# Two activations in one moving operand, and hidden tiles at a new place: the up and down projections of an MLP in a two-layer trunk on one core

## The chip, the core and the metric

The kernel runs on one core of one Trainium2 chip. Its engines are TensorE (matmuls and the loads of their stationary operand, PE and PEld in the profile), VectorE (DVE), ScalarE (ACT), GpSimd (POOL) and SyncE (SP, which issues most DMAs). The metric is the time of one execution on the device in microseconds (us).

## The reference

Two decoder layers over 256 tokens of width 2048, all in float32. Layer 0 mixes with a state-space block and an SSD block, layer 1 with RWKV-7 and RG-LRU; each layer then has an MLP and a gated embedding. What matters here, with the rest left out:

```python
def squared_relu_mlp(h, w1, w2):            # w1: 2048 x 8192, w2: 8192 x 2048
    return jnp.square(jax.nn.relu(h @ w1)) @ w2
...
    for i in range(2):
        hn = rmsnorm(h, norm_mix[i])
        ...
        h = h + mix
        h = h + squared_relu_mlp(rmsnorm(h, norm_ffn[i]), mlp_w1[i], mlp_w2[i])
        gate = jax.nn.sigmoid(rmsnorm(h, norm_pl[i]) @ pl_gate[i])
        h = h + gate * (p[i] @ pl_proj[i])
    return rmsnorm(h, norm_final)
```

## The kernel before

Every matmul of the large products takes its operands in a rounded float32 format (`FR`). To keep float32 accuracy each operand is split into a high part, the rounded value, and a low part, the rest; a product is then three matmuls, high by high, high by low and low by high, added in PSUM. The split is `split`: a copy on ScalarE (line 172) makes the high part, a subtraction on VectorE (line 153) the low one.

Weights stream from HBM in tiles of 512 KB, 128 partitions by 1024 values: `wload` issues the DMA on SP's queue into one of three `raw` buffers, `wtile_` splits it into `wh` and `wl`, which have three buffers each in layer 0 (`wp0`) and six in layer 1 from the last output projection on (`wp3`). They are given a high priority when the order of ScalarE's and VectorE's instructions is fixed at build time; each engine then works through its own list in that order.

Two helpers hold most of the matmuls. In `gemm_ws` (lines 344 to 362) the weights are stationary, 128x128 at a time, and the activations move, 256 tokens: the result has features on partitions. The MLP's up projection uses it, 512 columns of W1 per call, in two PSUM banks of the tag `acc` (six banks in the MLP). In `gemm_as` (lines 322 to 342) an activation tile of 128x128 is stationary and 512 weight columns move: the result has tokens on partitions. The MLP's down projection (`project`), the projection of the per-layer input (operand `px`) and the embed gate use it.

`prep` (from line 364) transposes the residual on TensorE (line 370) and splits it into the tiles that the matmuls read (`t` in the profile, from the pool `s4`). `mlp` (from line 455) runs over eight pieces c of 1024 hidden features: `up(c)` calls `gemm_ws` twice, and after each call ScalarE takes relu and square, and the result is split into the tiles `hid`; then the piece before is projected down with `project(prev, ...)`, four chunks of 512 output columns, each added to the residual on VectorE. In c = 0, where there is nothing to project yet, `between()` prepares `px` after the two calls.

Pools lie in SBUF one behind the other, in the order in which they are opened. In the MLP of layer 0 the weights' pool `wp0` comes first, then `h0` (four 4 KB tiles of the residual, 288 and 96 bytes), `pl0` (two `pt` tiles of 1 KB and two `px` tiles of 2 KB) and `mlp0`, which begins with the small tile `r2`, followed by the `hid` tiles of 4 KB. In layer 1 `pl1` follows `wp3` directly, and then `mlp1`. The pools `s4` and the weights' are a multiple of 512 bytes apart.

Of the kernel before, what the change touches and what calls it, by code (L numbers as in the profile page):

```python
# [11 lines left out]
F32 = mybir.dt.float32  # L12
FR = mybir.dt.float32r
I32 = mybir.dt.int32
AF = mybir.ActivationFunctionType
OP = mybir.AluOpType
# [3 lines left out]
D = 2048  # L20
T = 256
FF = 8192
# [49 lines left out]
class K:  # L72
# [249 lines left out]
    def gemm_as(self, xs, W, r0, c0, nn=512, shared=False):  # L322

        nk = len(xs)
        if shared:
            q = self.acc([128, 2, nn])
            ps = [q[:, 0], q[:, 1]]
        else:
            ps = [self.acc([128, nn]) for _ in range(2)]
        step = 2 * 512 // nn  # L330
        f = dict(skip_group_check=True)
        for kb in range(0, nk, step):
            wh, wl = self.wtile(W, r0[kb] if isinstance(r0, list) else r0 + kb, step, c0, nn)
            for kk in range(step):
                k = kb + kk
                h, l = xs[k]
                for t in range(2):
                    s = slice(128 * t, 128 * t + 128)
                    self.nc.tensor.matmul(ps[t], h[:, s], wh[:, kk], start=k == 0 and not (shared and t), stop=False, **f)  # L339
                    self.nc.tensor.matmul(ps[t], h[:, s], wl[:, kk], start=False, stop=False, **f)  # L340
                    self.nc.tensor.matmul(ps[t], l[:, s], wh[:, kk], start=False, stop=k == nk - 1, **f)  # L341
        return ps

    def gemm_ws(self, xs, W, c0, ms):
        nk = len(xs)
        nn = sum(ms)
        step = 4 if nn <= 256 else 2
        ps = [self.acc([128, 2, T]) for _ in range((len(ms) + 1) // 2)]
        for kb in range(0, nk, step):
            wh, wl = self.wtile(W, kb, step, c0, nn)  # L350
            for kk in range(step):
                k = kb + kk
                h, l = xs[k]
                o = 0
                for m, mw in enumerate(ms):
                    out = ps[m // 2][:mw, m % 2, :]
                    f = dict(skip_group_check=True)
                    self.nc.tensor.matmul(out, wh[:, kk, o:o + mw], h, start=k == 0 and m % 2 == 0, stop=False, **f)  # L358
                    self.nc.tensor.matmul(out, wh[:, kk, o:o + mw], l, start=False, stop=False, **f)  # L359
                    self.nc.tensor.matmul(out, wl[:, kk, o:o + mw], h, start=False, stop=k == nk - 1, **f)  # L360
                    o += mw
        return ps

    def prep(self, src, g, j0, nj, alloc=None):

        hb, lb = ((alloc or self.t4)([128, nj, T], FR) for _ in range(2))
        for i in range(nj):
            q = self.pq([128, T])
            for t in range(2):
                self.nc.tensor.transpose(q[:, 128 * t:128 * t + 128], src(t, j0 + i), self.ident)  # L370
            if g is None:
                self.split(hb[:, i], lb[:, i], q)
            else:
                s = g(j0 + i)
                self.pa = self.act(hb[:, i], q, AF.Copy, scale=s)
                self.pv = self.stt(lb[:, i], q, s, hb[:, i].bitcast(F32), OP.mult, OP.subtract)
                self.pas.append((self.pa, self.pv))
        return [(hb[:, i], lb[:, i]) for i in range(nj)]

    def norm_prep(self, gname):  # L380

# [64 lines left out]

        self.project([x for y, _ in ys for x in self.split_y(y)], W, [r + i for _, r in ys for i in range(4)], **k)

    def project(self, xs, W, r0, scale=None, nn=512):
        for c0 in range(0, D, nn):  # L450
            ps = self.gemm_as(xs, W, r0, c0, nn, nn < 512)
            for t in range(2):
                self.add_h(t, c0, ps[t], None if scale is None else scale[:, t:t + 1], nn)


    def mlp(self, i, w1, w2, between):

        xs, rstd = self.norm_prep(f"gf{i}")

        def up(c):  # L460
            hs = []
            for nb in range(2):
                ps = self.gemm_ws(xs, w1, c * 1024 + nb * 512, [128] * 4)
                hh, hl = (self.l("hid", 8, [128, 4, T], FR) for _ in range(2))
                for a in range(2):
                    r = self.l("relu", 4, [128, 2, T])
                    self.act(r, ps[a], AF.Relu)
                    self.act(r, r, AF.Square)
                    self.split(hh[:, 2 * a:2 * a + 2], hl[:, 2 * a:2 * a + 2], r)
                hs += [(hh[:, j], hl[:, j]) for j in range(4)]  # L470
            return hs

        prev = None
        with self.scope(f"mlp{i}") as self.lp:
            r2 = self.l("r2", 1, [128, 2])
            self.tt(r2, rstd, rstd, OP.mult)
            for c in range(FF // 1024 + 1):
                cur = up(c) if c < FF // 1024 else None
                if c == 0:
                    between()  # L480
                if prev is not None:
                    self.project(prev, w2, 8 * (c - 1), r2)
                prev = cur

    def embed_prep(self, i, p, pool):
# [7 lines left out]
    def embed(self, i, px, W, Wg, out=None):  # L493
        with self.scope(f"embed{i}") as self.lp:
            es = []
            for nb in range(4):
                pp = self.gemm_as(px, W, 0, 512 * nb)
                for t in range(2):
                    e = self.l("pl", 8, [128, 512])
                    self.act(e, pp[t], AF.Copy)  # L500
                    es.append(e)
            xs, rstd = self.norm_prep(f"gp{i}")

            def gate(t, c0, nn, ps):
                with (self.tc.high_priority(100000) if c0 >= 1536 else ExitStack()):
                    g = self.t2([128, 512], name="gate")[:, :nn]
                    self.act(g, ps, AF.Sigmoid, scale=rstd[:, t:t + 1])
                    e = es[2 * (c0 // 512) + t][:, c0 % 512:c0 % 512 + nn]
                    self.tt(g, g, e, OP.mult)
                    self.add_h(t, c0, g, nn=nn)  # L510
                    if out is not None:
                        self.final_part(t, c0, nn)

            for c0, nn in GB[:len(GB) - (out is not None)]:
                ps = self.gemm_as(xs, Wg, 0, c0, nn)
                for t in range(2):
                    gate(t, c0, nn, ps[t])
            if out is not None:

                c0, nn = GB[-1]  # L520
                ws = [self.wtile(Wg, kb, 1024 // nn, c0, nn) for kb in range(0, 16, 1024 // nn)]
                for t in range(2):
                    ps = self.acc([128, nn])
                    for k in range(16):
                        h, l = (x[:, 128 * t:128 * t + 128] for x in xs[k])
                        wh, wl = (w[:, k % (1024 // nn)] for w in ws[k // (1024 // nn)])
                        self.nc.tensor.matmul(ps, h, wh, start=k == 0, stop=False)
                        self.nc.tensor.matmul(ps, h, wl, start=False, stop=False)
                        self.nc.tensor.matmul(ps, l, wh, start=False, stop=k == 15)
                    gate(t, c0, nn, ps)  # L530
                    self.final(t, out)
# [287 lines left out]
    def ssd_dt(self, xs, rstd, raw):  # L819
        nc = self.nc  # L820
        hl = self.wp.tile([128, 16, 48], FR, name="wh", tag="wh")
        self.split(hl[:, :, 0:24], hl[:, :, 24:48], raw)
        q = self.pm([48, T])
        for k in range(16):
            h, l = xs[k]
            f = dict(skip_group_check=True)
            nc.tensor.matmul(q, hl[:, k], h, start=k == 0, stop=False, **f)
            nc.tensor.matmul(q[0:24], hl[:, k, 0:24], l, start=False, stop=k == 15, **f)
        d = self.t4([48, T], name="d")
        self.act(d, q, AF.Copy)  # L830
        pd = self.pm([128, 2, 24])
        for t in range(2):
            nc.tensor.matmul(pd[:, t], d[:, 128 * t:128 * t + 128], self.sel.bitcast(F32), start=True, stop=True)
        n = 48
        x = self.c([128, 48], pool=self.lp)
        for t in range(2):
            self.stt(x[:, 24 * t:24 * t + 24], pd[:, t], rstd[:, t:t + 1], self.hp[:, 0], OP.mult, OP.add)
        return x
# [665 lines left out]
```

## Time and profile before

| | |
|---|---|
| time of three runs, us | 2599.24, 2602.3, 2596.33 (median 2599.24) |
| profiled execution, its own time, us | 2599.46 |
| span of its instructions, us | 2597.7 |
| mean granted TensorE clock | 0.992 |
| instructions | 41093 |

The profile records one execution. The span is the time from the first to the last instruction. An engine's busy time counts its records without overlap; matmul records overlap, and their ends are modelled, so the pace of a run of matmuls is the difference of two start times divided by the number of steps between. L358 to L360 are the three matmuls of `gemm_ws`, L339 to L341 those of `gemm_as`. In the records `acc<-t,wh` names the output and the inputs by tile.

### The profile page before, as it was taken

To read this page: it belongs to the slowest core of one execution; us is meant where nothing else is said; L and a number is where in the kernel's file an instruction comes from. 1 tells how busy PE (TensorE), PEld (TensorE's weight loads), DVE (VectorE), ACT (ScalarE), POOL (GpSimd) and SP (SyncE) were. 2 spreads that over 40 slices of the span, in tenths; PEclk is the share of its full clock that TensorE was granted. 3 is DMA by queue.
4 is the path that set the end of the run, shared out by engine and by line. 5 is a ranking of instruction groups with operands and counts; after the bars stand their busy time and mean duration, and the time that the engine had idled before them with its cause. 6 is when DMAs were issued, how large, how long until landed. Compare 5 with 4: busy or idle time off the path is not lost. (4 is left out here: it accounts for less than half of the span.)

```text
span 2597.7 us, 41093 instructions
## 1 busy us (share of the span) xinstructions
PE 2538.0 (98%) x16352; PEld 2284.7 (88%) x16352; DVE 1630.8 (63%) x2557; ACT 1301.1 (50%) x1885; POOL 119.6 (5%) x255
## 2 busy tenths in 40 slices
PE   7989999999999999999999999999999999999998
PEld 6878878988988998878899998889898899889787
DVE  7999866455455445566566789775555545554565
ACT  5454745444444444455455667555444444444464
POOL 4200010000000000000100010100000000000000
PEclk9999999999999999999999999999999999999999
DMA  6545345665666566556556525366656656666654
GB/s 199 157 126 157 119 140 166 182 187 187 184 184 187 184 187 186 186 178 203 160 149 174 150 73 157 98 195 195 187 179 186 191 185 185 187 186 180 190 180 139
DMA packets 262593, 443.27 MB, mean 171 GB/s; under 512 B 16768, under 2 KB 81408, under 8 KB 262400
## 3 DMA queue, kind: packets, MB, share of 16 engines
q1 hardware_dynamic: 256560, 431.25, 54.6%
q0 software_dynamic: 5696, 9.18, 1.3%
q8 instruction: 128, 2.10, 0.3%
q14 instruction: 65, 0.53, 0.1%
q10 hardware_dynamic: 144, 0.21, 0.0%
HBM read 435.34 MB, written 5.24 MB: 170 GB/s over the span
## 5 line engine op out<-in xcount | busy, mean ns | idle before, releaser
L153 DVE TENSOR_TENSOR wl<-raw,wh 128x1024 fp32r<-128x1024 f32 x810 | 990.6, 1224 | 803.1 <-ACT wh L172 802.5
L172 ACT ACTIVATE wh<-raw 128x1024 fp32r<-128x1024 f32 x811 | 856.6, 1057 | 1063.1 <-PE acc L341 522.0
L360 PE MATMUL acc<-t,wl 128*128 128x256 f32 x3136 | 895.4, 286 | 9.2 <-DVE wl L153 9.0
L358 PE MATMUL acc<-t,wh 128*128 128x256 f32 x3136 | 895.8, 286 | 1.5 <-ACT t L172 1.1
L359 PE MATMUL acc<-t,wh 128*128 128x256 f32 x3136 | 895.7, 286 | 0.0
L360 PEld LDWEIGHTS acc<-t,wl 128*128 128x128 f32 x3136 | 603.8, 193 | 12.8 <-DVE wl L153 11.2
L358 PEld LDWEIGHTS acc<-t,wh 128*128 128x128 f32 x3136 | 603.8, 193 | 4.3 <-ACT t L172 1.3
L359 PEld LDWEIGHTS acc<-t,wh 128*128 128x128 f32 x3136 | 603.9, 193 | 2.2 <-issue 0.2
L340 PE MATMUL acc<-wl,hid 128*128 128x512 f32 x1024 | 407.0, 397 | 0.0
L339 PE MATMUL acc<-wh,hid 128*128 128x512 f32 x1024 | 404.9, 395 | 0.0
L341 PE MATMUL acc<-wh,hid 128*128 128x512 f32 x1024 | 404.2, 395 | 0.0
L339 PEld LDWEIGHTS acc<-wh,hid 128*128 128x128 f32 x1024 | 192.4, 188 | 46.9
L341 PEld LDWEIGHTS acc<-wh,hid 128*128 128x128 f32 x1024 | 192.3, 188 | 45.6
L340 PEld LDWEIGHTS acc<-wl,hid 128*128 128x128 f32 x1024 | 192.3, 188 | 44.1
L339 PE MATMUL acc<-wh,t 128*128 128x512 f32 (+1 forms) x480 | 179.7, 374 | 0.9 <-DVE fpad L153 0.9
L340 PE MATMUL acc<-wl,t 128*128 128x512 f32 (+1 forms) x480 | 179.9, 375 | 0.3 <-DVE wl L153 0.3
L341 PE MATMUL acc<-wh,t 128*128 128x512 f32 (+1 forms) x480 | 179.5, 374 | 0.0
L339 PEld LDWEIGHTS acc<-wh,t 128*128 128x128 f32 x480 | 91.5, 191 | 16.1 <-DVE fpad L153 1.1
L340 PEld LDWEIGHTS acc<-wl,t 128*128 128x128 f32 x480 | 91.6, 191 | 15.7 <-DVE wl L153 0.9
L341 PEld LDWEIGHTS acc<-wh,t 128*128 128x128 f32 x480 | 91.5, 191 | 14.7
L340 PE MATMUL acc<-wl,xh 128*128 128x256 f32 (+1 forms) x224 | 75.2, 336 | 1.5 <-DVE wl L153 1.5
L339 PE MATMUL acc<-wh,xh 128*128 128x256 f32 (+1 forms) x224 | 76.3, 341 | 0.0
(342 smaller groups left out, 2156.2 us busy)
## 6 DMA issues: line engine op xcount, KB each, us to landing
raw<-in_mlp_w SPq DMA_DIRECT2D x512, 512.0 KB, 3.7
raw<-in_o_in_proj SPq DMA_DIRECT2D x84, 512.0 KB, 3.7
raw<-in_e_in_proj SPq DMA_DIRECT2D x72, 512.0 KB, 3.7
raw<-in_pl_gate SPq DMA_DIRECT2D x64, 512.0 KB, 4.2
raw<-in_e_out_proj SPq DMA_DIRECT2D x32, 512.0 KB, 3.6
raw<-in_o_out_proj SPq DMA_DIRECT2D x32, 512.0 KB, 3.6
raw<-in_pl_proj SPq DMA_DIRECT2D x8, 512.0 KB, 3.8
c<-in_x SPq DMA_DIRECT2D x8, 256.0 KB, 7.2
```

The source lines that it names most:

```text
L153: self.ve.tensor_tensor(o, a, b, op=op)
L172: return self.nc.scalar.activation(o, a, f, **k)
L339: self.nc.tensor.matmul(ps[t], h[:, s], wh[:, kk], start=k == 0 and not (shared and t), stop=False, **f)
L340: self.nc.tensor.matmul(ps[t], h[:, s], wl[:, kk], start=False, stop=False, **f)
L341: self.nc.tensor.matmul(ps[t], l[:, s], wh[:, kk], start=False, stop=k == nk - 1, **f)
L358: self.nc.tensor.matmul(out, wh[:, kk, o:o + mw], h, start=k == 0 and m % 2 == 0, stop=False, **f)
L359: self.nc.tensor.matmul(out, wh[:, kk, o:o + mw], l, start=False, stop=False, **f)
L360: self.nc.tensor.matmul(out, wl[:, kk, o:o + mw], h, start=False, stop=k == nk - 1, **f)
```

## The change

The high and low parts of a `prep` tile now lie beside each other, so that one matmul can move both: 512 columns, 256 high and 256 low. A new helper, `gemm_wide`, serves the up projection: for each k-tile, four matmuls of 512 columns with the high weights of four column groups, then four of 256 columns with the low weights and the high activations. The sum high by low stands in the second half of each of four PSUM banks, and ScalarE and VectorE add it to the first half before relu. The two halves of an up piece alternate with the halves of the projection of the piece before. The tile `r2` is padded to 128 bytes in layer 0 and 512 bytes in layer 1. The other helpers read the first two of three members of a tile (`xs[k][:2]`), in four places of which one is shown.

```diff
--- before.py
+++ after.py
@@ -333,7 +333,7 @@
             wh, wl = self.wtile(W, r0[kb] if isinstance(r0, list) else r0 + kb, step, c0, nn)
             for kk in range(step):
                 k = kb + kk
-                h, l = xs[k]
+                h, l = xs[k][:2]
                 for t in range(2):
                     s = slice(128 * t, 128 * t + 128)
                     self.nc.tensor.matmul(ps[t], h[:, s], wh[:, kk], start=k == 0 and not (shared and t), stop=False, **f)
...
@@ -361,21 +361,39 @@
                     o += mw
         return ps
 
+    def gemm_wide(self, xs, W, c0, n):
+
+
+        ps = [self.acc([128, 2, T]) for _ in range(n)]
+        f = dict(skip_group_check=True)
+        for kb in range(0, len(xs), 2):
+            wh, wl = self.wtile(W, kb, 2, c0, 128 * n)
+            for kk in range(2):
+                h, _, hl = xs[kb + kk]
+                cs = [slice(128 * m, 128 * m + 128) for m in range(n)]
+                for m, s in enumerate(cs):
+                    self.nc.tensor.matmul(ps[m], wh[:, kk, s], hl, start=kb + kk == 0, stop=False, **f)
+                for m, s in enumerate(cs):
+                    self.nc.tensor.matmul(ps[m][:, 0], wl[:, kk, s], h, start=False, stop=kb + kk == len(xs) - 1, **f)
+        return ps
+
     def prep(self, src, g, j0, nj, alloc=None):
 
-        hb, lb = ((alloc or self.t4)([128, nj, T], FR) for _ in range(2))
+        hl = [(alloc or self.t4)([128, 2, 2, T], FR) for _ in range((nj + 1) // 2)]
+        xs = [hl[i // 2][:, i % 2] for i in range(nj)]
         for i in range(nj):
+            hi, lo = xs[i][:, 0], xs[i][:, 1]
             q = self.pq([128, T])
             for t in range(2):
                 self.nc.tensor.transpose(q[:, 128 * t:128 * t + 128], src(t, j0 + i), self.ident)
             if g is None:
-                self.split(hb[:, i], lb[:, i], q)
+                self.split(hi, lo, q)
             else:
                 s = g(j0 + i)
-                self.pa = self.act(hb[:, i], q, AF.Copy, scale=s)
-                self.pv = self.stt(lb[:, i], q, s, hb[:, i].bitcast(F32), OP.mult, OP.subtract)
+                self.pa = self.act(hi, q, AF.Copy, scale=s)
+                self.pv = self.stt(lo, q, s, hi.bitcast(F32), OP.mult, OP.subtract)
                 self.pas.append((self.pa, self.pv))
-        return [(hb[:, i], lb[:, i]) for i in range(nj)]
+        return [(x[:, 0], x[:, 1], x) for x in xs]
 
     def norm_prep(self, gname):
 
@@ -446,8 +464,8 @@
 
         self.project([x for y, _ in ys for x in self.split_y(y)], W, [r + i for _, r in ys for i in range(4)], **k)
 
-    def project(self, xs, W, r0, scale=None, nn=512):
-        for c0 in range(0, D, nn):
+    def project(self, xs, W, r0, scale=None, nn=512, cols=None):
+        for c0 in cols or range(0, D, nn):
             ps = self.gemm_as(xs, W, r0, c0, nn, nn < 512)
             for t in range(2):
                 self.add_h(t, c0, ps[t], None if scale is None else scale[:, t:t + 1], nn)
@@ -457,29 +475,35 @@
 
         xs, rstd = self.norm_prep(f"gf{i}")
 
-        def up(c):
-            hs = []
-            for nb in range(2):
-                ps = self.gemm_ws(xs, w1, c * 1024 + nb * 512, [128] * 4)
-                hh, hl = (self.l("hid", 8, [128, 4, T], FR) for _ in range(2))
-                for a in range(2):
-                    r = self.l("relu", 4, [128, 2, T])
-                    self.act(r, ps[a], AF.Relu)
-                    self.act(r, r, AF.Square)
-                    self.split(hh[:, 2 * a:2 * a + 2], hl[:, 2 * a:2 * a + 2], r)
-                hs += [(hh[:, j], hl[:, j]) for j in range(4)]
-            return hs
+        def up(c, nb):
+            ps = self.gemm_wide(xs, w1, c * 1024 + nb * 512, 4)
+            hh, hl = (self.l("hid", 8, [128, 4, T], FR) for _ in range(2))
+            for a in range(2):
+                r, q = self.l("relu", 4, [128, 2, T]), self.l("low", 2, [128, 2, T])
+                for j in range(2):
+                    p = ps[2 * a + j]
+                    self.act(q[:, j], p[:, 1], AF.Copy)
+                    self.tt(r[:, j], p[:, 0], q[:, j], OP.add)
+                self.act(r, r, AF.Relu)
+                self.act(r, r, AF.Square)
+                self.split(hh[:, 2 * a:2 * a + 2], hl[:, 2 * a:2 * a + 2], r)
+            return [(hh[:, j], hl[:, j]) for j in range(4)]
 
         prev = None
         with self.scope(f"mlp{i}") as self.lp:
-            r2 = self.l("r2", 1, [128, 2])
+
+            r2 = self.l("r2", 1, [128, 128 if i else 32])[:, 0:2]
             self.tt(r2, rstd, rstd, OP.mult)
             for c in range(FF // 1024 + 1):
-                cur = up(c) if c < FF // 1024 else None
-                if c == 0:
-                    between()
-                if prev is not None:
-                    self.project(prev, w2, 8 * (c - 1), r2)
+                cur = []
+                for nb in range(2):
+                    if c < FF // 1024:
+                        cur += up(c, nb)
+                    if c == 0 and nb:
+                        between()
+                    if prev is not None:
+                        for b in range(2 * nb, 2 * nb + 2):
+                            self.project(prev, w2, 8 * (c - 1), r2, cols=(512 * b,))
                 prev = cur
 
     def embed_prep(self, i, p, pool):
...
```

## Rows read from the trace of the kernel before

**Rows 1.** The page, busy time, share and instructions of TensorE.

```profile
PE 2538.0 (98%) x16352; PEld 2284.7 (88%) x16352; DVE 1630.8 (63%) x2557; ACT 1301.1 (50%) x1885; POOL 119.6 (5%) x255
```

**Rows 2.** Busy time by stretches, with records, granted clock, DMA share, GB/s.

```profile
core 0: us, PE busy (x) PEld busy (x) DVE busy (x) ACT busy (x) POOL busy (x), PEclk, DMA share, GB/s
...
657.70:748.40 90.70, 90.70 (x577) 81.94 (x577) 46.74 (x45) 40.28 (x44) 0.00 (x0) 1.00 0.61 185
...
2498.90:2563.90 65.00, 65.00 (x288) 53.83 (x287) 36.96 (x37) 32.65 (x40) 0.00 (x0) 1.00 0.63 200
```

**Rows 3.** Timeline of TensorE, layer 0: start and duration in us.

```profile
566.88 0.28 PE L358 MATMUL acc<-t,wh 128*128 128x256 f32 x1
...
612.94 0.39 PE L339 MATMUL acc<-wh,hid 128*128 128x512 f32 x1
...
657.74 0.28 PE L358 MATMUL acc<-t,wh 128*128 128x256 f32 x1
```

**Rows 4.** The same for layer 1.

```profile
1849.54 0.40 PE L339 MATMUL acc<-wh,hid 128*128 128x512 f32 x1
...
1894.33 0.28 PE L358 MATMUL acc<-t,wh 128*128 128x256 f32 x1
```

**Rows 5.** Timeline of TensorE, embed gate of layer 1.

```profile
2498.86 0.39 PE L339 MATMUL acc<-wh,t 128*128 128x512 f32 x1
...
2564.14 0.28 PE L339 MATMUL acc<-wh,t 128*128 128x256 f32 x1
...
2575.66 0.28 PE L527 MATMUL acc<-wh,t 128*128 128x256 f32 x1
```

**Rows 6.** The page, costliest groups, one of three alike.

```profile
L340 PE MATMUL acc<-wl,hid 128*128 128x512 f32 x1024 | 407.0, 397 | 0.0
```

**Rows 7.** Timeline of TensorE, projection of px in layers 0 and 1.

```profile
1164.00 0.39 PE L339 MATMUL acc<-wh,px 128*128 128x512 f32 x1
...
1168.18 0.40 PE L339 MATMUL acc<-wh,px 128*128 128x512 f32 x1
...
2493.20 0.39 PE L341 MATMUL acc<-wh,px 128*128 128x512 f32 x1
...
2495.46 0.39 PE L339 MATMUL acc<-wh,px 128*128 128x512 f32 x1
```

**Rows 8.** ScalarE's timeline, and groups of VectorE and ScalarE by shape.

```profile
478.16 0.37 ACT L172 ACTIVATE px<-pq 128x256 fp32r<-128x256 f32 x1
...
L153 DVE TENSOR_TENSOR h<-acc,h 128x256 f32<-128x256 f32 x32 | 12.4, 419 | 10.2 <-PE acc L341 10.2
...
L172 ACT ACTIVATE relu<-relu 128x512 f32<-128x512 f32 x64 | 40.3, 630 | 1.5
```

**Rows 9.** ScalarE's timeline in layer 0; the page's group of subtractions.

```profile
587.11 1.06 ACT L172 ACTIVATE wh<-raw 128x1024 fp32r<-128x1024 f32 x1 [1.82 <-PE acc L359]
589.38 0.60 ACT L172 ACTIVATE relu<-acc 128x512 f32<-128x512 f32 x1 [1.22 <-PE acc L360]
590.01 0.63 ACT L172 ACTIVATE relu<-relu 128x512 f32<-128x512 f32 x1
590.55 1.04 ACT L172 ACTIVATE wh<-raw 128x1024 fp32r<-128x1024 f32 x1
...
L153 DVE TENSOR_TENSOR wl<-raw,wh 128x1024 fp32r<-128x1024 f32 x810 | 990.6, 1224 | 803.1 <-ACT wh L172 802.5
```

**Rows 10.** Timelines of TensorE and ScalarE at a block's end.

```profile
474.73 0.28 PE L360 MATMUL acc<-t,wl 128*128 128x256 f32 x1
...
475.05 0.60 ACT L172 ACTIVATE relu<-acc 128x512 f32<-128x512 f32 x1 [1.22 <-PE acc L360]
```

**Rows 11.** Timeline of TensorE at the head of layer 0's MLP.

```profile
423.30 0.50 PE L358 MATMUL acc<-t,wh 128*128 128x256 f32 x2 [1.07 <-ACT t L172]
...
424.78 0.36 PE L359 MATMUL acc<-t,wh 128*128 128x256 f32 x1
```

**Rows 12.** ScalarE's timeline after a block of layer 1.

```profile
1802.51 0.60 ACT L172 ACTIVATE relu<-acc 128x512 f32<-128x512 f32 x1 [1.22 <-PE acc L360]
...
1806.24 2.01 ACT L172 ACTIVATE wh<-raw 128x1024 fp32r<-128x1024 f32 x2
```

More of the change, by code (lines that the diff above doesn't have):

```diff
@@ L352, in gemm_ws @@
                 k = kb + kk
-                h, l = xs[k]
+                h, l = xs[k][:2]
                 o = 0
@@ L524, in embed @@
                     for k in range(16):
-                        h, l = (x[:, 128 * t:128 * t + 128] for x in xs[k])
+                        h, l = (x[:, 128 * t:128 * t + 128] for x in xs[k][:2])
                         wh, wl = (w[:, k % (1024 // nn)] for w in ws[k // (1024 // nn)])
@@ L824, in ssd_dt @@
         for k in range(16):
-            h, l = xs[k]
+            h, l = xs[k][:2]
             f = dict(skip_group_check=True)
```

## The prediction, made before the changed kernel was run

> **What bounds the kernel now.** I read the page first: TensorE's share of the span, 98%, says that little can be won elsewhere [rows 1]. The table of stretches comes next: one cycle of the MLP (an up block pair and a projection, 657.7 to 748.4) has TensorE busy 90.70 of 90.70 us at a granted clock of 1.00, the 2.4 GHz level, with VectorE busy 46.74 and ScalarE 40.28 [rows 2]. Neither the weight stream nor the two helpers sets the time there. But "busy" is no measure of pace, because the records of neighbouring matmuls overlap. So the third view is TensorE's timeline at the borders between blocks, from which the pace is got by dividing.
>
> The up pair runs from 566.88 to 612.94: 46.06 us for 384 matmuls of 256 columns, 120.0 ns each. The projection that follows takes 44.80 us for 192 of 512 columns, 233.3 ns each [rows 3]. In layer 1 the projection takes 44.79 us, again 233.3 [rows 4]. The embed gate has the same form, 512 weight columns moving and an activation tile stationary, and it takes 2498.86 to 2564.14, 65.28 us for 288: 226.7 ns each; its 256-column part needs 11.52 us for 96, 120.0 ns [rows 5]. Two things follow. With well-placed operands the price of a matmul is linear: 256 more columns cost 106.7 ns, and 13.3 ns is fixed. And the projection after the MLP pays 6.6 ns per matmul over that line.
>
> **What the change removes and adds on TensorE.** *Up blocks.* There are 32 (two layers, 16 of 512 columns of W1), each with 16 k-tiles and 4 column groups: 2048 triples of 256 columns. A triple (wh by h, wh by l, wl by h) becomes one matmul of 512 columns and one of 256. Columns are unchanged; 2048 matmuls and their weight loads vanish. By rows 3 and 5 a triple goes from 3 x 120.0 = 360.0 to 226.7 + 120.0 = 346.7 ns. 13.3 x 2048 = 27.2 us. The trace has no 512-column moving activation against stationary weights from these pools. Bounds: 240.0 for the wide one (nothing won: it costs what two narrow ones cost) and 226.7 (the gate, whose roles are swapped); I take 226.7 because the narrow form costs 120.0 in either role, so the roles do not matter there. At 233.3, the projection's pace, the term is 13.7 us.
>
> *Projections.* The work is the same, 3072 matmuls (1024 on each of three lines) [rows 6]; only the place of `hid` changes. From tile sizes in the code, distances modulo 512 bytes: `s4`, which holds the gate's activations, lies 0 from the weights' pool. In layer 0 the small pool `h0` (288 + 96 bytes besides its big tiles) puts `pl0` 384 off, and `r2` (8 bytes, a 32-byte slot) puts `hid` 416 off. In layer 1 there is no `h0` between, and `hid` is 32 off. After the change `px` takes 4 KB more (no change modulo 512), and the padded `r2` of 128 and 512 bytes gives 384 + 128 = 512 and 512: distance 0 in both. What speaks for the place as the cause is `px`, whose projection is the same code in both layers: 384 off in layer 0, 18 steps from 1164.00 to 1168.18, 232.2 ns; 0 off in layer 1, 10 steps from 2493.20 to 2495.46, 226.0 ns [rows 7] (earlier ones in layer 1, just behind two waits, are slower, so a disturbance can hold the slow pace for a while). Three placements off, all near 233; two on, both near 226.7. 6.6 x 3072 = 20.3 us; if the place is not the cause, 0.
>
> A rule of the Trainium skill speaks against this term: the page "SBUF — State Buffer", section "Who interferes with whom", gives TensorE two independent read ports, one for the moving operand and one for weight loads, and says that it never waits on anyone. By it the place of a tile could not matter and the sum would lose this term; the two paces of `px` disagree with it.
>
> **What it adds on ScalarE and VectorE.** Each up block gets four copies of 128x256 out of PSUM (0.37 us, the `px` copy) and four additions (0.42 us, the 128x256 addition from `acc`); the relu reads SBUF (0.63 instead of 0.59) [rows 8]. Per cycle of two blocks: ScalarE 8 x 0.37 + 4 x 0.04 = 3.1 us more, VectorE 8 x 0.42 = 3.4 more, so some 43.4 and 50.1 of the new cycle of 87.9 us (128 x 0.3467 + 192 x 0.2267). Both hide behind TensorE as long as the weight splits come in time. How much time is there? In layer 0 there are three buffers: a `wh` copy starts when TensorE leaves a tile (ScalarE idle 1.82 us until L359) [rows 9], and then two tiles are ahead, 2 x 2.88 = 5.76 us, against copy 1.06 and subtraction 1.22 with some 0.03 between them: 3.4 us to spare. New tiles last 8 x 0.3467 = 2.77 or 12 x 0.2267 = 2.72 us, so 3.1 to spare. An evacuation now delays a copy by 590.55 - (587.11 + 2.88) = 0.56 us; ahead of it stood one relu and one square, 0.60 + 0.63 [rows 9]. After the change two copies, the wait for the second addition (some 0.5) and relu and square stand there: 0.74 + 0.5 + 1.26 = 2.5, or 1.3 more, 1.8 late in all. Hidden, with 1.3 left; without the cover every late microsecond is one on TensorE. In layer 1 six buffers leave five tiles, some 11.5 us. The weight stream must give 512 KB each 2.72 us; in the gate it does so already (200 GB/s, TensorE busy 65.00 of 65.00) [rows 2].
>
> **PSUM.** A block now holds four of six `acc` banks instead of two. Between blocks with projections in the rotation the bank six tiles back was left 10.9 us (48 x 0.2267) or more ago. Only in c = 0 does a block follow a block: its third group wants the bank of the one before's first group. The relu starts 0.04 us after the record of its last L360 (474.73 + 0.28) [rows 10]. With the four last narrow matmuls 0.12 apart, group 0's copy starts 0.16 before the new block and ends at +0.21, its addition at about +0.67, the second at +1.09; they are wanted at +0.45 and one matmul later. Stall about 0.45 us per layer; behind the transposes at c = 1 none. With a weight copy and a subtraction in front (1.06 + 1.22) it would be 2.7, twice per layer: 0 to 11 us, I take 1.
>
> **Head.** In the first block of each layer TensorE waits for the normalised tiles; two L358 start on the high part at 423.30, while the low one lets L359 start at 424.78 only [rows 11]. A wide matmul needs both, so 0.25 us of work moves behind the wait, and the block's own saving (0.85) may sink in other waits: 0 to 2.2 us for both layers, I take 1. The same transposes, copies and subtractions are issued in `prep`; where else it is used, their number stays. The halves of up and projection that now alternate change the order of the weight loads on SP's queue, not their number or size: 0.
>
> **Sum.** 27.2 + 20.3 - 1 - 1 = 45.5 us. Against the profiled execution's 2599.46 (span 2597.7, 1.8 around it; the median of the runs, 2599.24, is the same within 0.01%): 2554.0 us.
>
> **Rivals.**
> 1. *The place is not the cause* and `hid` stays at 233.3: 2599.5 - 27.2 + 2 = 2574. For it: the five placements differ in pool and in time as well, and the slow pace held for a while where `px` lay well. Against it: the two steady paces of `px`. The page on SBUF named above would give this. Chance 0.08.
> 2. *The wide matmul is not cheaper than, or only half as cheap as, two narrow ones* (240 or 233.3 ns): 2581 or 2568. For it: widths change every four matmuls, and in rows 7 the fast pace needed quiet before it came; against it: the borders of rows 3 cost nothing. Chance 0.09.
> 3. *The relay starves the split in layer 0 in part*: 1.3 us is a small rest, and each late microsecond there counts 16 times. At 1 us per block 2570, at 2 us 2586. Chance 0.05.
> 4. *The other side: the relay stands whole ahead of the weight copy.* ScalarE's order is fixed; if it holds all of a block's evacuation first, and each half's additions stand behind a subtraction, it is 4 x 0.37 + 2 x 1.88 + 2 x (1.22 + 0.84) = 9.4 us. The copy is due 0.6 after its start, so 8.8 late, 5.7 beyond the 3.1 to spare, in 16 blocks 91 us: 2645. It decides from 3.1 + 45.5/16 = 5.9 us late. For it: in layer 1 the order did put a whole evacuation (from 1802.51) ahead of two weight copies (1806.24) [rows 12]; against it: layer 0, with the short lead, has a weight copy after each square [rows 9]. Chance 0.03.
> 5. *No change*: gains eaten to within the 0.2% (about 5 us) that a measurement of this kernel can tell from none, by a mixture of 1, 2 and 3. Chance 0.02.
>
> **How the numbers follow.** The forecast has the remaining 0.73, with 2549 to 2560 as its own range (nothing lost, down to the 47.5 of the two terms and a little; or 4 us more of stalls). To leave out no more than 2 in 10 the range takes in rivals 1, 2 and the lighter half of 3: 2548 to 2582. Faster 0.94 (forecast, 1, 2 and nearly all of 3), same 0.03, slower 0.03.
>
> **What the changed profile would show.** TensorE's timeline in an up block: groups of four records of 512 columns 0.227 apart, then four of 256 columns 0.120 apart; a block in 22.2 us. The `hid` matmuls 0.227 apart in both layers. No idle time of TensorE ahead of wh or wl in layer 0. Two short waits for an addition where c = 0. VectorE and ScalarE about 54 and 50 us busier in all. Wrong would be: steps of 0.233 in either place, TensorE waiting for a subtraction once per block, or a gap at each change of width.

## The result, and the profile after

| | before | changed |
|---|---|---|
| median, us | 2600.68 (2596.33 to 2602.3, 4 runs) | 2566.04 (2565.65 to 2566.57, 4 runs) |
| ratio, 95% interval | | 0.9869 [0.9855, 0.9882] |
| profiled span, us | 2597.7 | 2564.7 |

The change gains 34.6 us by the medians, 33.0 by the two profiled spans; 45.5 were forecast. The time lies inside the stated range of 2548 to 2582, but 12 us above its likeliest point of 2554, close to the 2568 that rival 2 gave for a wide matmul at the slow pace.

The page of the changed kernel, busy time and the groups that answer to [rows 1, 6]; columns as there:

```profile
PE 2503.9 (98%) x14304; PEld 2175.0 (85%) x14304; DVE 1676.1 (65%) x2685; ACT 1334.3 (52%) x2013; POOL 114.5 (4%) x255
...
L375 PE MATMUL acc<-t,wh 128*128 128x512 f32 x2048 | 563.9, 395 | 0.0
...
L340 PE MATMUL acc<-wl,hid 128*128 128x512 f32 x1024 | 399.5, 390 | 0.0
```

2048 matmuls are gone (16352 to 14304). TensorE's timeline at the borders of a block, the answer to [rows 3]; "x4" is a merged group of four:

```profile
606.77 1.07 PE L375 MATMUL acc<-t,wh 128*128 128x512 f32 x4
607.68 0.64 PE L377 MATMUL acc<-t,wl 128*128 128x256 f32 x4
608.15 1.09 PE L375 MATMUL acc<-t,wh 128*128 128x512 f32 x4
609.08 0.63 PE L377 MATMUL acc<-t,wl 128*128 128x256 f32 x4
609.55 1.09 PE L375 MATMUL acc<-t,wh 128*128 128x512 f32 x4
610.48 0.64 PE L377 MATMUL acc<-t,wl 128*128 128x256 f32 x4
610.96 1.09 PE L375 MATMUL acc<-t,wh 128*128 128x512 f32 x4
...
629.20 0.40 PE L339 MATMUL acc<-wh,hid 128*128 128x512 f32 x1
...
651.00 1.07 PE L375 MATMUL acc<-t,wh 128*128 128x512 f32 x4
```

The first four wide matmuls of the block take 607.68 - 606.77 = 0.91 us, 227 ns each, as forecast. The second four, behind four narrow ones, take 0.93 us, 232.5 each, and so do the rest. A whole block takes 22.43 us instead of 23.03 (half of 46.06 [rows 3]); 22.19 were forecast. Half a projection, 96 matmuls, takes 21.80 us, 227.1 each, instead of 233.3.

So the account, 32 blocks x 0.60 = 19.2 us and 16 projections x (44.80 - 43.60) = 19.2 us, makes 38.4. From the last matmul ahead of each MLP to its last `hid` matmul the two traces differ by 18.0 us in layer 0 and 17.6 in layer 1, 35.6: the pieces c = 0, heads included, give back the other 2.8. Outside the MLPs the changed execution is 2.6 longer in all; what is known of that is told at the end.

ScalarE after a block of layer 0, the answer to [rows 9], and the table of stretches for half a projection, the answer to [rows 2]:

```profile
628.92 1.06 ACT L172 ACTIVATE wh<-raw 128x1024 fp32r<-128x1024 f32 x1 [1.75 <-PE acc L375]
629.89 1.19 ACT L172 ACTIVATE low<-acc 128x256 f32<-128x256 f32 x4
631.94 0.63 ACT L172 ACTIVATE relu<-relu 128x512 f32<-128x512 f32 x1 [0.87 <-DVE relu L153]
632.48 1.04 ACT L172 ACTIVATE wh<-raw 128x1024 fp32r<-128x1024 f32 x1
```

```profile
629.50:651.10 21.60, 21.60 (x97) 17.86 (x96) 14.10 (x17) 12.13 (x18) 0.00 (x0) 1.00 0.62 194
```

In the block shown all four copies stand together, then ScalarE waits 0.87 us for the additions. The weight copy due at 628.92 + 2.81 = 631.73 starts at 632.48, 0.75 late, and TensorE stays busy 21.60 of 21.60 us.

### The profile page after: what moved, and what is told of

It is laid out like the page before. It is cut to its first block, busy times and chain, and to the rows that moved or that the text cites. A ratio compares the mean times of both kernels' runs of the same rounds, so it can differ in the third digit from the quotient of the medians.

```text
span 2564.7 us, 37322 instructions
## 1 busy us (share of the span) xinstructions
PE 2503.9 (98%) x14304; PEld 2175.0 (85%) x14304; DVE 1676.1 (65%) x2685; ACT 1334.3 (52%) x2013; POOL 114.5 (4%) x255
## 5 line engine op out<-in xcount | busy, mean ns | idle before, releaser
L375 PE MATMUL acc<-t,wh 128*128 128x512 f32 x2048 | 563.9, 395 | 0.0
L341 PE MATMUL acc<-wh,hid 128*128 128x512 f32 x1024 | 400.1, 391 | 0.0
L339 PE MATMUL acc<-wh,hid 128*128 128x512 f32 x1024 | 399.1, 390 | 0.0
L375 PEld LDWEIGHTS acc<-t,wh 128*128 128x128 f32 x2048 | 351.5, 189 | 48.4 <-DVE relu L153 0.8
L377 PEld LDWEIGHTS acc<-t,wl 128*128 128x128 f32 x2048 | 315.9, 189 | 43.7
L377 PE MATMUL acc<-t,wl 128*128 128x256 f32 x2048 | 329.3, 281 | 0.0
L360 PE MATMUL acc<-t,wl 128*128 128x256 f32 (+1 forms) x1088 | 316.6, 292 | 8.9 <-DVE wl L153 8.7
L359 PE MATMUL acc<-t,wh 128*128 128x256 f32 (+1 forms) x1088 | 316.6, 291 | 0.0
L358 PE MATMUL acc<-t,wh 128*128 128x256 f32 (+1 forms) x1088 | 316.5, 291 | 0.0
L360 PEld LDWEIGHTS acc<-t,wl 128*128 128x128 f32 (+1 forms) x1088 | 211.5, 195 | 12.5 <-DVE wl L153 10.8
L358 PEld LDWEIGHTS acc<-t,wh 128*128 128x128 f32 (+1 forms) x1088 | 211.8, 195 | 2.0 <-ACT wh L172 0.4
L359 PEld LDWEIGHTS acc<-t,wh 128*128 128x128 f32 (+1 forms) x1088 | 211.6, 194 | 1.7 <-issue 0.2
L339 PEld LDWEIGHTS acc<-wh,t 128*128 128x128 f32 x480 | 90.9, 189 | 15.8 <-DVE fpad L153 1.1
```

Source lines behind the costliest of these rows:

```text
L375: self.nc.tensor.matmul(ps[m], wh[:, kk, s], hl, start=kb + kk == 0, stop=False, **f)
L377: self.nc.tensor.matmul(ps[m][:, 0], wl[:, kk, s], h, start=False, stop=kb + kk == len(xs) - 1, **f)
```

## The experiments

Theory 1: a wide matmul costs 227 ns when matmuls of its own width ran before it, and about five are slowed behind a change from narrow to wide. Theory 2: a wide moving activation costs 233 in any order. A second question is whether the place of `hid` is what took the projection from 233 to 227. The code differences are shortened: "wide" and "narrow" stand for the two lines with the matmuls of 512 and 256 columns. The ratio is to runs of the kernel before that were taken beside the run.

| run | time, us | ratio to before, 95% interval |
|---|---|---|
| changed, first | 2566.04 | 0.9869 [0.9855, 0.9882] |
| changed_again | 2566.76 | 0.9875 [0.986, 0.9889] |
| eights | 2562.29 | 0.9859 [0.9845, 0.9874] |
| sixteens | 2563.12 | 0.9859 [0.9844, 0.9874] |
| alternate | 2566.0 | 0.9868 [0.9852, 0.9885] |
| whole_pieces | 2566.4 | 0.9868 [0.9852, 0.9885] |
| no_pad | 2579.19 | 0.9925 [0.9911, 0.994] |
| pad_only | 2579.99 | 0.9928 [0.9911, 0.9944] |
| off_place | 2572.82 | one run |
| apart_128 | 2566.75 | one run |
| all_wide | 2770.43 | one run |

**all_wide: no change of width inside a block.**

```diff
-self.nc.tensor.matmul(ps[m][:, 0], wl[:, kk, s], h, ...)
+self.nc.tensor.matmul(ps[m], wl[:, kk, s], hl, ...)
```

> Changed kernel, but the low weights are multiplied by high and low activations too, 512 columns, so no width changes inside a block (a fourth product, low by low, is added, and 2048 matmuls get 256 columns more). Theory 1: all wide steps at 227 ns, a block of 128 in 29.0 us, about 2566 + 32 x (29.0 - 22.5) = 2774. Theory 2: steps of 233 throughout, 29.9 us, about 2803.

TensorE's timeline inside a block:

```profile
641.37 1.07 PE L375 MATMUL acc<-t,wh 128*128 128x512 f32 x4
642.28 1.07 PE L377 MATMUL acc<-t,wl 128*128 128x512 f32 x4
643.19 1.07 PE L375 MATMUL acc<-t,wh 128*128 128x512 f32 x4
...
664.04 1.07 PE L377 MATMUL acc<-t,wl 128*128 128x512 f32 x4
```

25 groups of four in 664.04 - 641.37 = 22.67 us: 226.7 ns each. 2770.43 us against 2774 and 2803. The role of the operands and the four banks cost nothing; theory 2 falls.

**eights and sixteens: longer runs of one width.** The loops over the k-tiles and the column groups stand inside each width; the sixteens take two weight tiles at a time.

```diff
-for kk in range(2):
-    for m, s in enumerate(cs): wide
-    for m, s in enumerate(cs): narrow
+for kk in range(2):
+    for m, s in enumerate(cs): wide
+for kk in range(2):
+    for m, s in enumerate(cs): narrow
```

> Changed kernel, but with the eight wide matmuls of a weight tile ahead of its eight narrow ones, instead of four and four twice. Theory 1 (a change from narrow to wide costs: 227 ns per wide matmul in the first group of a block, 228 to 236 in the groups behind a narrow one, some 18 ns per group in sum): half as many changes, so 4 to 5 us faster than the changed kernel's 2566, if the slow pace heals within a group; 2566 if it lasts through it. Theory 2 (a wide moving activation costs 233 in any order, for its role or its four banks): 2566 and wide steps near 233 in all positions but the block's first four.

> As the eights, but over two weight tiles: sixteen wide matmuls, then sixteen narrow ones. The eights showed that behind a narrow one about five wide ones are slow (233, 236, 228, 233, 231) and the rest run at 227, some 20 ns per change with the narrow ones' gain taken off. Theory 1: 3 changes per block instead of 7 (eights) and 15 (changed kernel), so 28 fewer per... 32 blocks x 4 x 20 ns = 2.6 us faster than the eights, 7.7 faster than the changed kernel: 2558 to 2560. If holding two weight tiles at a time starves TensorE in layer 0, where there are three buffers: slower than the eights, with waits of TensorE for wl in layer 0 alone.

TensorE's timeline of the eights:

```profile
607.77 1.98 PE L374 MATMUL acc<-t,wh 128*128 128x512 f32 x8
609.59 1.12 PE L377 MATMUL acc<-t,wl 128*128 128x256 f32 x8
610.54 2.00 PE L374 MATMUL acc<-t,wh 128*128 128x512 f32 x8
612.38 1.12 PE L377 MATMUL acc<-t,wl 128*128 128x256 f32 x8
...
616.13 2.00 PE L374 MATMUL acc<-t,wh 128*128 128x512 f32 x8
...
630.09 0.40 PE L339 MATMUL acc<-wh,hid 128*128 128x512 f32 x1
```

And of the sixteens:

```profile
609.66 3.79 PE L374 MATMUL acc<-t,wh 128*128 128x512 f32 x16
...
615.20 3.82 PE L374 MATMUL acc<-t,wh 128*128 128x512 f32 x16
...
620.77 3.82 PE L374 MATMUL acc<-t,wh 128*128 128x512 f32 x16
...
631.90 0.40 PE L339 MATMUL acc<-wh,hid 128*128 128x512 f32 x1
```

From its first matmul to the projection behind it a block takes 629.20 - 606.77 = 22.43 us in the changed kernel, 630.09 - 607.77 = 22.32 in the eights and 631.90 - 609.66 = 22.24 in the sixteens; without changes it would take 64 x (226.7 + 120.0) ns = 22.19. The excess is 0.24, 0.13 and 0.05 us for 15, 7 and 3 changes from narrow to wide: 16, 19 and 17 ns per change. In the eights the wide ones behind a change step by 233, 236, 228, 233, 231 and then 227, 227, 227 (medians of the timeline by position): the slow pace heals. The first narrow one behind a wide one gives 7 ns back (113 instead of 120).

From the last matmul ahead of each MLP to its last `hid` matmul, both layers together, it is 1433.1 us in the changed kernel, 1430.0 in the eights and 1427.4 in the sixteens: 3.1 and then 2.6 us less, where 4 to 5 and 2.6 were expected. No wait of TensorE for wl shows in the steady part, so two weight tiles at a time starve nothing. But the sixteens are the only kernel here in which a wide matmul waits for an addition on VectorE to leave a PSUM bank, once, in the first piece of layer 1 (the page, idle time in the last column):

```profile
L374 PE MATMUL acc<-t,wh 128*128 128x512 f32 x2048 | 492.8, 392 | 0.7 <-DVE relu L153 0.7
```

The times agree in direction (2566 to 2562 and 2563), but the runs of these kernels scatter by more than that (the eights from 2560.55 to 2568.02), and the sixteens' are not below the eights': the gain is shown by the traces alone.

**alternate: a change at every matmul.**

```diff
-for m, s in enumerate(cs): wide
-for m, s in enumerate(cs): narrow
+for m, s in enumerate(cs): wide; narrow
```

> Changed kernel, but ungrouped: each wide matmul is followed by its narrow one, so every matmul changes width. Theory 1: four times as many changes; the step of a wide and a narrow together goes from 351 to between 354 (each wide 236, each narrow 118) and 365 ns, so 2572 to 2594. Theory 2: the pair stays at 351, 2566.

```profile
609.67 0.40 PE L375 MATMUL acc<-t,wh 128*128 128x512 f32 x1
609.91 0.28 PE L376 MATMUL acc<-t,wl 128*128 128x256 f32 x1
...
613.91 0.40 PE L375 MATMUL acc<-t,wh 128*128 128x512 f32 x1
```

Twelve pairs in its timeline take 4.24 us, 353.3 each, against 351 in fours. The wide steps are 236 (median), the narrow ones behind them 117: a narrow one gives back 3 ns. With a single wide matmul behind each change, a change costs 353.3 - 346.7 = 6.6 ns. The two MLPs take 1436.5 us instead of 1433.1, yet the time is 2566.0, below the 2572 that I gave as the lower end; in its profile the stretch between the MLPs is 3.7 us shorter (597.2 against 600.9), for which see the last section. Grouping by four is worth 3.3 us in the two MLPs by the traces, and not visible in the runs.

**no_pad and pad_only: the place of hid, undone and alone.**

```diff
 no_pad (from the changed kernel)
-r2 = self.l("r2", 1, [128, 128 if i else 32])[:, 0:2]
+r2 = self.l("r2", 1, [128, 2])
 pad_only (from the kernel before)
-r2 = self.l("r2", 1, [128, 2])
+r2 = self.l("r2", 1, [128, 128 if i else 32])[:, 0:2]
```

> Changed kernel with r2 not padded, so that the hidden tiles lie 416 and 32 bytes off a multiple of 512 from the weights again. If their place is the cause of the projection's 233.3 ns before: its steps go back from 227 to 233 and the time to 2566 + 20 = 2586. If the alternating halves or something else in the change is the cause: steps of 227, 2566.

> The kernel before with r2 alone padded as in the change, so hidden tiles 0 bytes off a multiple of 512 from the weights and everything else as before. If the place term stands by itself: projection steps of 227 in both layers, 3072 x 6.1 = 18.7 us faster than before, 2581. If it needs the other parts of the change (the alternating halves, the other neighbours): 2600.

A projection in TensorE's timeline, no_pad and then pad_only, first and last of 12 steps:

```profile
639.79 0.40 PE L339 MATMUL acc<-wh,hid 128*128 128x512 f32 x1
...
642.59 0.40 PE L339 MATMUL acc<-wh,hid 128*128 128x512 f32 x1
```

```profile
640.17 0.39 PE L339 MATMUL acc<-wh,hid 128*128 128x512 f32 x1
...
642.89 0.39 PE L339 MATMUL acc<-wh,hid 128*128 128x512 f32 x1
```

2.80 / 12 = 233.3 ns without the padding, 2.72 / 12 = 226.7 with it and nothing else. Padding a tile of eight bytes takes 20.9 us off the kernel before (2600.84 to 2579.99); by the traces 18.7 of them lie in the two MLPs (9.4 and 9.3), as expected. Without it the changed kernel is 13.2 us slower instead of 20: the two MLPs are 9.2 and 8.8 us longer by the traces, and the stretch between them is 5.0 shorter (595.9 against 600.9).

The kernel before with the padding also shows what [rows 3] could not, the projection's start behind an up block of 256 columns:

```profile
611.59 0.40 PE L339 MATMUL acc<-wh,hid 128*128 128x512 f32 x1
...
612.75 0.39 PE L341 MATMUL acc<-wh,hid 128*128 128x512 f32 x1
...
613.88 0.39 PE L340 MATMUL acc<-wl,hid 128*128 128x512 f32 x1
```

The first five steps take 1.16 us, 232 each, the next five 1.13, 226 each. So the slow start behind narrow matmuls is there without `gemm_wide` too.

**off_place: other distances.**

```diff
-r2 = self.l("r2", 1, [128, 128 if i else 32])[:, 0:2]
+r2 = self.l("r2", 1, [128, 160 if i else 96])[:, 0:2]
```

> Changed kernel with r2 padded by 256 bytes more in layer 0 and 128 more in layer 1: hidden tiles 256 and 128 bytes off a multiple of 512 from the weights. If only a multiple of 512 bytes is fast: steps of 233 in both layers. If a multiple of 256 does: 227 in layer 0, 233 in layer 1. If place does not matter: 227 in both.

Layer 0 (256 bytes off), then layer 1 (128 bytes off), 12 steps each in TensorE's timeline:

```profile
639.61 0.39 PE L339 MATMUL acc<-wh,hid 128*128 128x512 f32 x1
...
642.33 0.39 PE L339 MATMUL acc<-wh,hid 128*128 128x512 f32 x1
...
1899.76 0.39 PE L340 MATMUL acc<-wl,hid 128*128 128x512 f32 x1
...
1902.54 0.40 PE L340 MATMUL acc<-wl,hid 128*128 128x512 f32 x1
```

226.7 at 256 bytes; 231.7 at 128 in these twelve steps, 232.9 in the mean of that layer's projections. A multiple of 256 is enough here; of the distances tried, those that leave 32, 128 (128 and 384) or 160 (416) modulo 256 are slow.

**apart_128: the other activations moved off.** A tile of 128 bytes between `s4` and the weights' pool.

```diff
+k.gap = k.s1.tile([128, 32], F32, name="gap", tag="gap")
+nc.gpsimd.memset(k.gap, 0.0)
```

> Changed kernel with a tile of 128 bytes between the pool of the activations and that of the weights: all activation tiles 128 bytes off, the hidden tiles still 0 off. If the place of any stationary tile against the moving one counts: gate steps from 227 to 233, the wide matmuls slow in the block's first group too (233 instead of 227), hidden steps at 227. If only the hidden tiles are touched by it: all steps as in the changed kernel.

TensorE's timeline, a block and then 12 steps of the gate of layer 1:

```profile
607.15 1.09 PE L375 MATMUL acc<-t,wh 128*128 128x512 f32 x4
608.08 0.64 PE L377 MATMUL acc<-t,wl 128*128 128x256 f32 x4
608.55 1.10 PE L375 MATMUL acc<-t,wh 128*128 128x512 f32 x4
...
609.96 1.09 PE L375 MATMUL acc<-t,wh 128*128 128x512 f32 x4
...
2500.01 0.39 PE L341 MATMUL acc<-wh,t 128*128 128x512 f32 x1
...
2502.81 0.39 PE L341 MATMUL acc<-wh,t 128*128 128x512 f32 x1
```

The gate goes from 226.7 [rows 5] to 233.3 ns, and the block's first wide group from 0.91 to 0.93 us; the hidden steps stay at 227. So it holds for either role. The weights and `hid` have moved together here and stay fast, while the gate's tiles have stayed where they were and are slow: what counts is the distance between the two operands, not the address of either alone. Behind a change of width the place is worth almost nothing, 1.40 to 1.41 us per k-tile with it and without.

**whole_pieces: a block behind a block in every piece.**

```diff
-for nb in range(2): cur += up(c, nb); two chunks of project(prev)
+cur = up(c, 0) + up(c, 1); all four chunks of project(prev)
```

> Changed kernel without the alternating halves: both up blocks of a piece, then all four chunks of the projection, so in every piece a block follows a block and its third column group wants a PSUM bank that the block before has just left. By the prediction's price 14 more such borders cost 0.45 us each: 6 us, 2572. If the order of TensorE's instructions goes around the wait, as it does at the first border of the changed kernel (two column groups for some k-tiles, no wait in the trace), the cost is only the added changes of width, some 4 per border at 20 ns: about 1 us, 2567.

2566.4 us: 14 more such borders cost nothing that can be measured (both MLPs together take 1433.2 us, against 1433.1), and the waits of TensorE show none in the steady part of either MLP. The changed kernel's own first border shows why, in TensorE's timeline:

```profile
450.40 0.64 PE L377 MATMUL acc<-t,wl 128*128 128x256 f32 x4
450.88 0.63 PE L375 MATMUL acc<-t,wh 128*128 128x512 f32 x2
451.34 0.39 PE L377 MATMUL acc<-t,wl 128*128 128x256 f32 x2
451.57 0.62 PE L375 MATMUL acc<-t,wh 128*128 128x512 f32 x2
```

For several k-tiles two of the four groups go ahead, in an order fixed at build time. The records do not name the groups; that they are the two whose banks are free is read from the code.

**changed_again.** The changed kernel once more.

> The changed kernel unchanged, beside the sixteens on the same chip. In its first profile the stretch between the two MLPs took 600.9 us, in all others 595.7 to 597.2, with stretches at a granted clock of 0.57 to 0.61. If those clock drops belong to that one execution: stretch of 596 to 597 us and a span near 2560 to 2561. If they belong to the kernel: 600.9 again, span near 2564.7. The times should repeat 2566 either way.

2566.76 us, a span of 2565.8, and the stretch between the MLPs at 600.7 us: the longer stretch came in both profiled executions of this kernel.

## Why the prediction was right or wrong

**The bound** was right: TensorE stayed the bound (98%), and nearly all of the gain is a pace of its matmuls.

**Up blocks, 27.2 us forecast, 19.2 measured:** the step that failed. The mechanism, a matmul and a load less per triple, was right; the size hung on "I take 226.7 because the narrow form costs 120.0 in either role". The role indeed does not matter (all_wide). But the rows for 226.7 come from a stretch in which every matmul has one width, and the change makes 15 changes from narrow to wide per block: 32 x 15 x 16 ns = 7.7 us, nearly all of the 8.0 missing. Rival 2 had named the changes of width, and I set against it that "the borders of rows 3 cost nothing": those borders do not show it, because the one from narrow to wide led into a projection that was slow anyway; with the padding alone its first five steps are slow (pad_only). That the time still lies in the range is owed to rival 2, whose 2568 the range took in; the forecast's own 2549 to 2560 missed it.

**Projections, 20.3 us forecast, 19.2 measured:** right, and the cause is shown: undone, alone, at other distances, and with other tiles. Rival 1 falls. Two chunks at 227.1 instead of 226.7 carry the same slow start behind a block. What I had drawn from the page "SBUF — State Buffer" of the Trainium skill (section "Who interferes with whom"), that place could not matter, is contradicted by 233.3 against 226.7 ns in no_pad and pad_only. I had worked with multiples of 512 bytes; 256 serve as well. What in the memory or the array makes it so was not tried.

**ScalarE and VectorE, nothing forecast, nothing measured:** right. The copies are 380 ns and the additions 415, as taken, but overlap: busy time grew by 33.2 and 45.3 us instead of 50 and 54, and the weight copy came 0.75 us late, not 1.8. Rivals 3 and 4 fall.

**PSUM and head, 2 us forecast, 2.8 given back in c = 0:** the size is near, in part by luck, because the mechanism of the PSUM half did not come. No wait for a bank appears in the changed kernel; the order goes around it. Only the sixteens show one, of 0.7 us in layer 1, where 0.45 per layer were forecast. How the 2.8 us divide between changed order, changes of width and the head (one wait of 2.4 us for the low part of a tile in layer 0 where 1.1 and 0.8 stood before) is open.

**Left out:** 2.6 us that the profiled execution lost outside the MLPs, told below.

## What to carry to other kernels

Take a matmul's price from a stretch with the same neighbours, not only the same shape: here five wide matmuls behind a narrow one paid 1 to 9 ns each. Longer runs of one width gained 3.1 and then 2.6 us of 2566 in the traces, too little to show in the runs. Before joining or reordering matmuls, compare the pace of equal forms in different pools; padding one eight-byte tile was worth as much (18.7 us in the MLPs, pad_only) as removing 2048 matmuls (19.2). And pace is a difference of start times: busy time stood at 98% before and after.

## What the runs showed of the hardware that was not expected

The place of the stationary tile against the moving one (modulo 256 bytes) and the width of the matmul before both set the pace: 6.6 ns in 227 for the place, and 16 to 19 ns per change in runs of four to sixteen matmuls (6.6 where every matmul changes). They do not add: behind a change a badly placed operand costs next to nothing more (apart_128).

Outside the MLPs, where the changed kernel and the eights have the same code, whole microseconds moved. The same stretch of layer 1's mixer, the changed kernel and then the eights, in the table of stretches:

```profile
1533.00:1541.00 8.00, 8.00 (x40) 7.25 (x40) 4.41 (x9) 4.00 (x7) 0.10 (x1) 0.57 0.00 0
```

```profile
1533.00:1541.00 8.00, 7.82 (x60) 6.81 (x59) 7.18 (x14) 7.21 (x17) 0.10 (x1) 1.00 0.24 61
```

The granted clock is 0.57 in one, most of it at the 1.2 GHz level, and 1.00 in the other; TensorE does 40 matmuls instead of 60, though it was busy 9.94 of 10 us in the stretch from 1520 in both. In the changed kernel's two profiles, the sixteens' and whole_pieces' the stretch between the MLPs takes 600 to 601 us with this drop, in the kernel before and the eights 596 without it. All of these have another drop earlier in that mixer (in the changed kernel a granted clock of 0.61 from 1253 to 1257); apart_128, with the later drop alone, takes 598.9, and pad_only, with neither, 594.7. The chip alone does not decide it: off_place ran beside the sixteens on the same chip and is without the later drop (597.5). So some 3 to 4 us of the difference between these profiled executions has nothing to do with the MLP, and in them it hides what the sixteens gain. Each kernel but the changed one has a single profile, so how often the drop comes in each is open, and so is what lets the clock fall there.
